# Taps and operand sums one product later, operand tiles at one offset from the weights, and an ordered end of the last stage

## The chip, the cores and the metric

The kernel runs on one core of a Trainium2 chip. The metric is the device time of one execution in microseconds (us). TensorE (PE) multiplies, VectorE (DVE) and ScalarE (ACT) do elementwise work, SyncE (SP) issues most transfers, and GpSimd (POOL) issues the transfers that add to what is already in the destination.

## The reference, cut to what matters

One layer of a hybrid encoder on 512 tokens of 2048 channels, float32:

```python
h = rms_norm(x, norm_mix_w); proj = h @ w_in            # attention and gated linear attention
x = x + concat([y_a, y_g]) @ w_out                      # stage "wo"
h = rms_norm(x, norm_ffn_w)
u = causal_depthwise_conv(h @ w_ffn_up, w_conv, b_conv) # stage "up": width 3, 2 * 5632 channels
u_gate, u_val = split(u, 2)
x = x + (gelu(u_gate) * u_val) @ w_ffn_down             # stages "dn0", "dn1", "dn2"
h = rms_norm(x, norm_ple_w)
x = x + sigmoid(h @ w_ple_gate) * (p @ w_ple_proj)      # stage "pg"
out = rms_norm(x, final_norm_w)
```

## The kernel before, in words

**Two parts.** Up to about 630 us the kernel does the input projection and both kinds of attention. Then `p @ w_ple_proj` is made ("pp"), and the six stages above follow as one list of steps. Only this list and its end are touched by the change, apart from where some tiles lie.

**Units and products.** A stage is a list of units: wo 8, up 44, dn0, dn1 and dn2 8 each, pg 8, 84 in all. A unit makes two blocks of 128 output channels for two halves of 256 tokens, a two-by-two block product with seven multiplications in place of eight. The seven products P1, P2, P6, P5, P7, P3, P4 (lines 29 to 31) each take a combination of weight blocks (L11, L12, S2, S1, S3, S4, L22) and one of seven operands (R11, R21, N2, N1, T3, R22, T4). The last unit of pg has the order P1, P2, P6, P7, P4, P5, P3 (`HALVES`), so that its first token half is finished two products early. `product` (line 736) does 3 matmuls of 128x256 for each block of 128 inputs, high by high, high by low, low by high: 24 matmuls, or 21 in dn1 and dn2. The sums lie in three PSUM banks A, B and C. `collect` (line 755) moves a product out of its bank: the first of a quarter by ACT (P1, P6, P5, P4), the others by DVE (P2, P7, P3). A product that goes into a bank again has to wait until the last `collect` of this bank is done.

**What is done around a product.** At step i the program first does `prep(i + 2)` (line 714): a sum of weight blocks by DVE where one is needed ("s"), the high part of the weights by ACT ("wh") and the low part by DVE ("wl"). Then come the 24 matmuls of step i, then what the `agenda` has for this step, then `collect`. "wh" and "wl" have three pages each, so "wh" of step i+2 can't start before product i-1 is done. In the six stages PE, ACT and DVE run in program order (`InOrder`, line 54); the issue of transfers by SP and POOL is put in order by the framework.

**After a unit of up** (`after_up`, line 833), in the steps of the next unit. In the first step (P1): `scale` by DVE (u <- u,rb) and the last tap of both halves by ACT (cv <- u,cw). In the second (P2): two taps of the gate half by DVE. In the third (P6): GELU by ACT and two taps of the other half by DVE. In the fourth (P5): the product of both halves by DVE, and for every second unit `store_pair` (line 536): four operand sums by DVE (tp) and seven stores to DRAM (g_R, g_N, g_T). The first unit of such a pair leaves its result in its page until then.

**After a unit of pg** the gate is applied (`gate_steps`), the squares go to `acc`, and the result is stored (x3d). In the last unit six of these blocks are read back and weighted by ACT (`weigh`, 12 instructions of 128x512). Its end (lines 983 to 1002) is not in program order: mean square, square root, reciprocal and spreading over the partitions for each token half, a multiplication by DVE for each of 8 blocks, and 16 stores of 256 KB.

**Where tiles lie.** Weight pages "wh" and "wl" are 4096 bytes of each partition, a block of 128 columns is 512 bytes. The operand tiles are 8192 bytes; R11, R21 and N2 lie in the pool `xa` (line 523), which is laid from the top of the memory down, below the pool `late` (line 522); N1, T3, R22 and T4 lie in the pool `xb` (line 574) behind the pages and a tile `pad` of 32 bytes. In the allocation of the kernel before, every weight page begins at byte 3136 of a 4096-byte block, every `xb` tile at 3168, every `xa` tile at 4064; `xb` ends 896 bytes below `xa`. The attention part has tiles of its own in the same space: h, 4096 bytes each, begins at byte 3136 like the pages.

Of the kernel before, what the change touches and what calls it, by code (L numbers as in the profile page):

```python
# [39 lines left out]
def encoder_block(ctx: ExitStack, tc: tile.TileContext, A, out):  # L40
# [115 lines left out]
    def rstd_tok(parts, n, dst):  # L156
        nt = parts[0].shape[1] // P
        ms = psum_aux("ms")
        for t in range(nt):
            for i, sumsq in enumerate(parts):  # L160
                nc.tensor.matmul(ms[:, t:t + 1], sumsq[:, t * P:(t + 1) * P], ones[:, 0:1],
                                 start=i == 0, stop=i == len(parts) - 1)
        w = tp.tile([P, 3 * TT], F32, tag="tok", name="tok")
        a, y, t = w[:, 0:nt], w[:, TT:TT + nt], w[:, 2 * TT:2 * TT + nt]
        nc.vector.tensor_scalar(a, ms[:, 0:nt], 1.0 / n, EPS, ALU.mult, ALU.add)
        nc.scalar.activation(y, a, AF.Sqrt)
        nc.vector.reciprocal(y, y)
        nc.vector.tensor_tensor(t, y, y, ALU.mult)
        nc.vector.scalar_tensor_tensor(t, t, -0.5, a, ALU.mult, ALU.mult)
        nc.vector.scalar_tensor_tensor(dst, t, 1.5, y, ALU.add, ALU.mult)  # L170

    def rstd_bc(rt):
        nt = rt.shape[1]
        dg = tp.tile([P, T], F32, tag="dg", name="dg", bufs=1)
        for t in range(nt):
            nc.vector.tensor_scalar(dg[:, t * P:(t + 1) * P], ident, rt[:, t:t + 1], None, ALU.mult)
        pb = psum_aux("pb")[:, :nt * P]
        nc.tensor.matmul(pb, ones, dg[:, :nt * P], start=True, stop=True)
# [343 lines left out]
    late.append(ctx.enter_context(tc.tile_pool(name="late", bufs=1, side="right", reuse_waits="tile")))  # L522
    xa = ctx.enter_context(tc.tile_pool(name="xa", bufs=1, side="right", reuse_waits="tile"))
# [212 lines left out]
    def product(unit, prod):  # L736
# [9 lines left out]
        for k in range(kb):  # L746
            x = st.x[op, k // 4]
# [85 lines left out]
    def after_up(unit):  # L833
# [41 lines left out]
    def after_gate(unit):  # L875
        return gate_steps(unit) + [(3, lambda: nc.sync.dma_start(x3d[unit.u], unit.xs))]
# [67 lines left out]
    for m in range(6):  # L944
        agenda[end + 4 + m // 3].append((2, lambda m=m: weigh(m)))
# [9 lines left out]
    for i, (unit, prod) in enumerate(steps):  # L955
# [8 lines left out]
        prep(i + 2)  # L964
        product(unit, prod)
        for k, f in todo:
            if k:
# [3 lines left out]
        if unit is units[-1] and j == 6:  # L971
            for e in (vec, act, ten):
# [92 lines left out]
```

## Time and profile before

| | |
|---|---|
| time before, median of 3 runs | 2454.15 us (2450.79 to 2454.41) |
| the profiled execution's own time | 2446.06 us |
| its span, first to last instruction | 2444.3 us |
| mean granted clock of TensorE | 0.986 |
| first product of wo, up, dn0, dn1, dn2, pg | 671.0, 832.8, 1762.8, 1937.8, 2083.3, 2231.1 us |

The profile shows one execution. A row of the timeline holds: start in us, length in us, engine, line, operation, out <- in, tile, count, and in brackets how long the engine sat idle before it and what ended this. The in-order engines are recorded under line 62, since a helper issues their instructions; rows are told apart by their tiles (up_T is T3 or T4, up_R is R11, R21 or R22, by bank A, B or C). Matmuls overlap and their ends are modelled, so their pace is read from their starts. PEclk is the granted clock as a share of full speed.

### The profile page before, as it was taken

The page shows a single profiled execution, that of the slowest core. Times are in us where ns is not written, and L with a number is a line of the kernel's source. Part 1 is how long each engine was busy: PE and PEld are TensorE (multiplying, and loading weights), DVE is VectorE, ACT ScalarE, POOL GpSimd, SP SyncE. Part 2 cuts the span into 40 slices and gives each one's busy share as a digit, 9 for nine tenths or more (in the row PEclk, how much of TensorE's full clock was granted, in tenths as well). Part 3 has the DMA queues.
Part 4 walks back from the last instruction along what each step waited for, and adds up shares of the span by engine and source line. Part 5 has one row for each costly group of instructions (what it writes and reads, how often), then busy time and mean ns, then how long its engine had stood idle before and what let it go on. Part 6 is the DMA issues. An engine that isn't in the chain of part 4 may idle for free.

```text
span 2444.3 us, 42306 instructions
## 1 busy us (share of the span) xinstructions
PE 2346.1 (96%) x16904; PEld 2182.8 (89%) x16904; DVE 1795.8 (73%) x2436; ACT 1231.2 (50%) x1770; POOL 103.4 (4%) x133
## 2 busy tenths in 40 slices
PE   9999999999999899999999999999989999898995
PEld 8878887777799899999999999999989999898895
DVE  5355336665588888878878787878887887999786
ACT  6344235554465654554554545544554544656554
POOL 0000000000000000000000000000000000000000
PEclk9999999999999999999999999999989999999997
DMA  5222222223987967777777777777854846769564
GB/s 198 85 78 74 99 95 95 91 91 123 305 278 231 324 172 199 206 200 195 201 195 201 197 206 195 203 195 208 269 192 156 286 155 212 276 213 328 166 215 163
DMA packets 171653, 462.72 MB, mean 189 GB/s; under 512 B 18720, under 2 KB 62496, under 8 KB 171456
## 3 DMA queue, kind: packets, MB, share of 16 engines
q1 hardware_dynamic: 152288, 396.58, 46.3%
q0 software_dynamic: 16992, 61.35, 13.9%
q8 instruction: 132, 2.16, 0.3%
q10 hardware_dynamic: 2176, 2.10, 0.3%
q14 instruction: 65, 0.53, 0.1%
HBM read 383.41 MB, written 69.21 MB: 185 GB/s over the span
## 4 chain that ended last, share of the span: by engine, by line
PE 60%; DVE 17%; ACT 8%; issue 8%; DMA 6%; SPq 0%; ACTq 0%; DVEq 0%
PE accA L62 21%; PE accC L62 10%; DVE wl L62 5%; ACT wh L62 4%; PE accB L62 4%; DVE u L62 3%; DMA g_N<-tp 3%; DVE cv L62 3%; PE v L241 2%; PE v L242 2%; PE v L243 2%; DVE s L62 2%; ACT cv L62 1%; PE pqa L124 1%; PE pqa L123 1%
## 5 line engine op out<-in xcount | busy, mean ns | idle before, releaser
L62 DVE TENSOR_TENSOR wl<-s,wh 128x1024 fp32r<-128x1024 f32 (+1 forms) x304 | 364.9, 1200 | 249.5 <-ACT wh L62 247.0
L62 ACT ACTIVATE wh<-l 128x1024 fp32r<-128x1024 f32 (+1 forms) x284 | 294.0, 1035 | 247.3 <-PE accC L62 130.4
L62 DVE TENSOR_TENSOR wl<-l,wh 128x1024 fp32r<-128x1024 f32 (+1 forms) x284 | 338.7, 1193 | 42.9 <-ACT wh L62 40.7
L62 ACT ACTIVATE wh<-s 128x1024 fp32r<-128x1024 f32 (+1 forms) x304 | 310.2, 1034 | 36.7 <-DVE s L62 32.8
L62 PE MATMUL accA<-up_T,wh 128*128 128x256 f32 x1408 | 255.8, 281 | 12.6 <-DVE u L62 12.4
L62 PEld LDWEIGHTS accA<-up_T,wh 128*128 128x128 f32 x1408 | 215.9, 189 | 16.6 <-issue 16.2
L62 ACT ACTIVATE u<-accA 128x256 f32<-128x256 f32 x253 | 95.2, 376 | 257.7 <-PE accA L62 256.2
L62 PE MATMUL accA<-up_T,wl 128*128 128x256 f32 x704 | 201.6, 286 | 5.3
L62 DVE TENSOR_TENSOR s<-s,l 128x1024 f32<-128x1024 f32 (+1 forms) x168 | 200.6, 1194 | 4.8 <-DMA l<-in_w_out 2.7
L62 PEld LDWEIGHTS accA<-up_T,wl 128*128 128x128 f32 x704 | 132.9, 189 | 13.7 <-DVE wl L62 13.7
L62 PE MATMUL accA<-up_N,wh 128*128 128x256 f32 x704 | 132.6, 289 | 3.8 <-ACT u L62 3.4
L62 DVE SCALAR_TENSOR_TENSOR cv<-u,cw,cv 128x511 f32<-128x511 f32 (+1 forms) x176 | 131.7, 748 | 3.1
L62 PE MATMUL accA<-up_R,wh 128*128 128x256 f32 x704 | 128.9, 283 | 4.6 <-DVE up_R L62 2.3
L62 PE MATMUL accA<-dn_T,wh 128*128 128x256 f32 x704 | 127.5, 281 | 1.8 <-DVE dn_T L62 1.8
L62 PE MATMUL accB<-up_R,wh 128*128 128x256 f32 x704 | 128.2, 282 | 0.2 <-DVE up_R L62 0.2
L62 PE MATMUL accC<-up_N,wh 128*128 128x256 f32 x704 | 125.6, 279 | 1.8 <-DVE up_N L62 1.8
L62 PE MATMUL accC<-up_R,wh 128*128 128x256 f32 x704 | 125.5, 279 | 0.1
L62 ACT ACTIVATE cv<-u,cw 128x512 f32<-128x512 f32 x88 | 67.0, 809 | 110.3 <-DVE u L62 110.3
L62 PEld LDWEIGHTS accA<-up_N,wh 128*128 128x128 f32 x704 | 108.7, 190 | 10.9 <-ACT u L62 6.0
L62 PEld LDWEIGHTS accA<-up_R,wh 128*128 128x128 f32 x704 | 108.9, 190 | 5.5 <-DVE up_R L62 2.5
L676 POOL DMA_DIRECT2D s<-in_w_up x88 | 75.0, 852 | 852.1 <-DMA s<-in_w_up 423.5
L62 PEld LDWEIGHTS accA<-dn_T,wh 128*128 128x128 f32 x704 | 108.3, 189 | 3.0 <-DVE dn_T L62 2.8
(369 smaller groups left out, 6486.9 us busy)
## 6 DMA issues: line engine op xcount, KB each, us to landing
l<-in_w_up SPq DMA_DIRECT2D x132, 512.0 KB, 6.5
s<-in_w_up SPq DMA_DIRECT2D x88, 512.0 KB, 4.2
s<-in_w_up POOLq DMA_DIRECT2D x88, 512.0 KB, 7.2
l<-in_w_dn SPq DMA_DIRECT2D x60, 448.0 KB, 5.0
l<-in_w_ple_gate SPq DMA_DIRECT2D x32, 512.0 KB, 5.8
l<-in_w_out SPq DMA_DIRECT2D x30, 512.0 KB, 5.5
l<-in_w_dn SPq DMA_DIRECT2D x30, 512.0 KB, 4.9
g_R<-cv SPq DMA_DIRECT2D x66, 128.0 KB, 6.6
```

Of the source, the lines that this page charges most:

```text
L62: ins = f(*args, **kw)
L123: nc.tensor.matmul(po, whi, act[:, 0, :], start=start, stop=False)
L124: nc.tensor.matmul(po, whi, act[:, 1, :], start=False, stop=False)
L241: nc.tensor.matmul(ps[t], h1[kt][:, 0, sl], wh, start=kt == 0, stop=False)
L242: nc.tensor.matmul(ps[t], h1[kt][:, 0, sl], wl, start=False, stop=False)
L243: nc.tensor.matmul(ps[t], h1[kt][:, 1, sl], wh, start=False, stop=kt == KD - 1)
L676: nc.gpsimd.dma_start(t, src("L22" if name == "S1" else "L11"), accum_op=ALU.add)
```

## The change

The two taps by ACT go from the first step to the second, and the operand sums with their stores (`join`) from the fourth to the fifth. A tile `shim` of 960 bytes is put into the pool `late`, ahead of `xa`. The tile "rt" with its two buffers of 32 bytes, which lay below the weight pages, is no longer there. At the end, all three engines stay in program order to the last instruction; the last product is cut after 5 of its 8 blocks for the mean square of the first token half; two of the eight blocks are weighted in the final multiplication and no longer by ACT; the other weightings are spread over more steps; the store of the last but one unit, which nothing read, is left out.

```diff
     late.append(ctx.enter_context(tc.tile_pool(name="late", bufs=1, side="right", reuse_waits="tile")))
+    shim = late[0].tile([P, 240], F32, tag="shim", name="shim")
+    nc.gpsimd.memset(shim, 0.0)
     xa = ctx.enter_context(tc.tile_pool(name="xa", bufs=1, side="right", reuse_waits="tile"))
...
-    def product(unit, prod):
+    def product(unit, prod, at=None, between=None):
...
         for k in range(kb):
+            if k == at:
+                between()
...
         def gate():
             g = unit.c[:, 1, :]
             vec.tensor_tensor(g, unit.c[:, 0, :], g, ALU.mult)
+
+        def join():
             ci, k, second = unit.slot
-            if not second:
-                held[0] = g
+            if second:
+                store_pair(gd[ci], k, held[0], unit.c[:, 1, :])
             else:
-                store_pair(gd[ci], k, held[0], g)
-
-        return [(0, scale), (0, lambda: tap(0, 2)), (0, lambda: tap(1, 2)), (1, lambda: [tap(0, 1), tap(0, 0)]),
+                held[0] = unit.c[:, 1, :]
+
+        return [(0, scale), (1, lambda: [tap(0, 2), tap(1, 2)]), (1, lambda: [tap(0, 1), tap(0, 0)]),
                 (2, lambda: act.activation(unit.c[:, 0, :], unit.c[:, 0, :], AF.Gelu_apprx_tanh)),
-                (2, lambda: [tap(1, 1), tap(1, 0)]), (3, gate)]
+                (2, lambda: [tap(1, 1), tap(1, 0)]), (3, gate), (4, join)]
...
     def after_gate(unit):
-        return gate_steps(unit) + [(3, lambda: nc.sync.dma_start(x3d[unit.u], unit.xs))]
+        keep = [] if unit is units[-2] else [(3, lambda: nc.sync.dma_start(x3d[unit.u], unit.xs))]
+        return gate_steps(unit) + keep
...
-    for m in range(6):
-        agenda[end + 4 + m // 3].append((2, lambda m=m: weigh(m)))
+    for m in range(4):
+        agenda[end + 3 + m // 2].append(((1, 3, 1, 1)[m], lambda m=m: weigh(m)))
...
+        if i == len(steps) - 1:
+            break
         product(unit, prod)
         for k, f in todo:
-            if k:
+            if 0 < k < 3:
                 f()
         if j == 6 and unit.first and st.chained:
             rstd_wide(acc, D, rb)
-        if unit is units[-1] and j == 6:
-            for e in (vec, act, ten):
-                e.on = False
         collect(unit, prod)
+        for k, f in todo:
+            if k == 3:
+                f()
         if unit is units[-1]:
             if prod == "P4":
-                for _, f in gate_steps(unit, lo_half):
+                for n, (_, f) in enumerate(gate_steps(unit, lo_half)):
                     f()
+                    if n == 1:
+                        weigh(4)
...
-    pb0 = rms_tokens([acc[:, lo_half]])
-    for _, f in gate_steps(unit, hi_half):
-        f()
-    pb1 = rms_tokens([acc[:, hi_half]])
-    for m in (6, 7):
-        x3[m] = units[m - 8].xs
-        weigh(m)
-    finish(lo_half, pb0)
-    finish(hi_half, pb1)
+    def finish(c, pb, ms):
+        for m in ms:
+            t = x3[m][:, :, c]
+            if m < 6:
+                vec.tensor_tensor(t, t, pb[:, None, :].broadcast_to([P, 2, 256]), ALU.mult)
+            else:
+                for s in range(2):
+                    vec.scalar_tensor_tensor(t[:, s, :], t[:, s, :], nfin[:, m + 8 * s:m + 8 * s + 1], pb,
+                                             ALU.mult, ALU.mult)
             (nc.sync if m % 2 else nc.scalar).dma_start(out2[m][:, :, c], t)
+    got = []
+    product(unit, prod, 5, lambda: got.append(mean_square(lo_half)))
+    w0 = rstd_begin(got[0])
+    collect(unit, prod)
+    x3[6], x3[7] = units[-2].xs, unit.xs
+    c = hi_half
+    o, xs = unit.o[:, :, c], unit.xs[:, :, c]
+    vec.tensor_tensor(o, o, rb[:, None, c].broadcast_to([P, 2, 256]), ALU.mult)
+    act.activation(o, o, AF.Sigmoid)
+    weigh(5)
+    r0 = rstd_end(w0)
+    pb0 = spread(r0, lo_half)
+    vec.tensor_tensor(o, o, unit.pp[:, :, c], ALU.mult)
+    vec.tensor_tensor(xs, xs, o, ALU.add)
+    sqs = []
+    for s in range(2):
+        q = tp.tile([P, T], F32, tag="sq", name="sq")[:, c]
+        act.activation(q, xs[:, s, :], AF.Square)
+        sqs.append(q)
+    finish(lo_half, pb0, range(1))
+    for q in sqs:
+        vec.tensor_tensor(acc[:, c], acc[:, c], q, ALU.add)
+    ms1 = mean_square(hi_half)
+    finish(lo_half, pb0, range(1, 2))
+    w1 = rstd_begin(ms1)
+    finish(lo_half, pb0, range(2, 3))
+    r1 = rstd_end(w1)
+    pb1 = spread(r1, hi_half)
+    finish(lo_half, pb0, range(3, 8))
+    finish(hi_half, pb1, range(8))
```

`mean_square` is two matmuls of `acc` with a column of ones, `rstd_begin` one DVE instruction and the square root by ACT, `rstd_end` four small DVE instructions, `spread` two DVE instructions and one matmul.

More of the change, by code (lines that the diff above doesn't have):

```diff
@@ L175, in rstd_bc @@
         for t in range(nt):
[L176 removed]
+            vec.tensor_scalar(dg[:, t * P:(t + 1) * P], ident, rt[:, t:t + 1], None, ALU.mult)
         pb = psum_aux("pb")[:, :nt * P]
[L178 removed]
+        ten.matmul(pb, ones, dg[:, :nt * P], start=True, stop=True)
         return pb
@@ new lines, in rstd_end, with spread @@
+    def rstd_end(w):
+        a, y, t, r = (w[:, 2 * q:2 * q + 2] for q in range(4))
+        vec.reciprocal(y, y)
+        vec.tensor_tensor(t, y, y, ALU.mult)
+        vec.scalar_tensor_tensor(t, t, -0.5, a, ALU.mult, ALU.mult)
+        vec.scalar_tensor_tensor(r, t, 1.5, y, ALU.add, ALU.mult)
+        return r
+    def spread(r, c):
+        dg = tp.tile([P, T], F32, tag="dg", name="dg", bufs=1)[:, c]
+        for t in range(2):
+            vec.tensor_scalar(dg[:, t * P:(t + 1) * P], ident, r[:, t:t + 1], None, ALU.mult)
+        tag = 3 * ((unit.index + 1) % 2) + c.start // 256
+        pb = pp_.tile([P, T], F32, tag=f"b{tag}", name="pb")[:, :256]
+        ten.matmul(pb, ones, dg, start=True, stop=True)
+        return pb
```

31 lines of the change are left out of this document (17 added, 14 removed).

## The prediction

> **What bounds the kernel now.** I read the page first, then the timeline of PE alone, then those of DVE and ACT in the same stretches. The page says 96% for PE, but a matmul's length is modelled, so I go by starts. Four steps of a unit of wo (the fourth row is the start of P5), then the start of the next unit:
>
> ```profile
> 753.48 0.40 PE L62 MATMUL accA<-wo_R,wh 128*128 128x256 f32 x2
> 756.36 0.40 PE L62 MATMUL accB<-wo_R,wh 128*128 128x256 f32 x2
> 759.24 0.40 PE L62 MATMUL accA<-wo_N,wh 128*128 128x256 f32 x2
> 762.12 0.40 PE L62 MATMUL accC<-wo_N,wh 128*128 128x256 f32 x2
> 773.32 0.40 PE L62 MATMUL accA<-wo_R,wh 128*128 128x256 f32 x2
> ```
>
> Nothing waits here. P1, P2 and P6 take 2.88 us each, the other four (773.32 - 762.12) / 4 = 2.80. That is 120.0 against 116.7 ns for a matmul of one form, and the slow three read the tiles of `xa`. A unit takes 19.84 us; with seven fast products it would take 19.60.
>
> Now up: the starts of its third unit and of dn0, and between them one pair of units (P1, P7, P3, P4, then the next two P1).
>
> ```profile
> 890.95 0.40 PE L62 MATMUL accA<-up_R,wh 128*128 128x256 f32 x2
> ...
> 1015.43 0.40 PE L62 MATMUL accA<-up_R,wh 128*128 128x256 f32 x2
> ...
> 1026.96 0.39 PE L62 MATMUL accA<-up_T,wh 128*128 128x256 f32 x2
> ...
> 1030.16 0.39 PE L62 MATMUL accC<-up_R,wh 128*128 128x256 f32 x2
> ...
> 1033.70 0.47 PE L62 MATMUL accA<-up_T,wh 128*128 128x256 f32 x2 [0.57 <-DVE u L62]
> ...
> 1036.57 0.40 PE L62 MATMUL accA<-up_R,wh 128*128 128x256 f32 x2
> ...
> 1056.91 0.40 PE L62 MATMUL accA<-up_R,wh 128*128 128x256 f32 x2
> ...
> 1762.83 0.39 PE L62 MATMUL accA<-dn_R,wh 128*128 128x256 f32 x2
> ```
>
> The pair takes 41.48 us (21.14 + 20.34) against 39.20 at full pace. P7 takes 1030.16 - 1026.96 = 3.20, so it waits 0.40 inside; P4 starts 3.54 after P3, so it waits 0.74 for DVE's `collect`. All 42 units from the third on take 871.88 us, 20.76 each. PE is the bound in wo and dn; in up the order of DVE and ACT costs it over 1 us a unit. The rows of the second unit (ACT, then DVE, then three DVE rows of the pair's first):
>
> ```profile
> 1040.54 1.52 ACT L62 ACTIVATE cv<-u,cw 128x512 f32<-128x512 f32 x2 [2.43 <-DVE u L62]
> 1041.96 0.36 ACT L62 ACTIVATE u<-accA 128x256 f32<-128x256 f32 x1
> 1042.23 2.00 ACT L62 ACTIVATE wh<-s 128x1024 fp32r<-128x1024 f32 x2
> ```
>
> ```profile
> 1039.28 1.22 DVE L62 TENSOR_TENSOR u<-u,rb 128x1024 f32<-128x1024 f32 x1
> 1043.31 1.23 DVE L62 TENSOR_TENSOR wl<-s,wh 128x1024 fp32r<-128x1024 f32 x1 [2.80 <-ACT wh L62]
> ...
> 1047.36 1.22 DVE L62 TENSOR_TENSOR wl<-s,wh 128x1024 fp32r<-128x1024 f32 x1
> ```
>
> ```profile
> 1030.53 0.76 DVE L62 TENSOR_TENSOR tp<-cv 128x256 f32<-128x256 f32 x2
> ...
> 1033.14 0.41 DVE L62 TENSOR_TENSOR u<-u,accA 128x256 f32<-128x256 f32 x1
> ```
>
> ACT waits 2.43 us for `scale`, does both taps, only then collects P1 and makes wh of P5; DVE, done with `scale` at 1040.5, sits idle 2.80 us for that wh. The lost time comes back as P7's wait: its wl starts at 1047.36, and P7 is due 11.3 us after 1036.57, at 1047.9. In the pair's other unit the four operand sums and one wl hold DVE from 1030.53 to 1033.14, so `collect` of P7 comes late for P4.
>
> **The taps and the sums.** Nothing is added: two taps (0.76 us each) move from step P1 to step P2 on ACT, four sums from P5 to P7 on DVE. I write out a unit from its start 0, with products 2.80 long, DVE at 1.15 between starts of 128x1024 instructions, 0.76 a tap and 1.00 for a wh. P2 starts at 2.80, P6 5.60, P5 8.40, P7 11.20, P3 14.00, P4 16.80. ACT: `collect` P1 at 3.0, wh of P5 3.3 to 4.3, taps 4.3 to 5.8, wh of P7 to 6.8, GELU when its taps are there, 7.0 to 7.8. DVE: `scale` 2.7 to 3.9, wl of P5 4.3 to 5.5, two taps to 7.0, `collect` P2 7.4, s to 8.5, wl of P7 8.5 to 9.7 (due 11.4), two taps to 11.2, wl of P3 12.4 (due 14.2), gate 13.0, wl of P4 14.2. Then in every second unit the sums, 1.46, to 15.7, and `collect` P7 to 16.0, due 16.8. The next wl are done at 17.2 and 19.7, due 19.8 and 22.6. Nothing is late; the smallest slack is the 0.8 us at P4. The total doesn't bind either:
>
> ```profile
> 990.28:1745.02 754.74, 739.17 (x6110) 722.92 (x6109) 607.85 (x729) 374.29 (x507) 61.33 (x72) 1.00 0.72 202
> ```
>
> Over these 36 units of up (columns PE, weight loads, DVE, ACT, POOL, clock, DMA share, GB/s) DVE works 607.85 / 754.74 = 0.81 of the time, 33.4 us of a pair, and 39.2 are there.
>
> So each of the 42 units comes to 19.60 us if the operands are all fast: 871.88 - 823.2 = **48.7**. If the `xa` operands stay slow, up to 0.24 a unit is left as in wo, 10 us in all; in the unit of 20.34 only 0.34 is over when 19.60 and P7's 0.40 are taken off, with other small waits in it, so I take half, 5 us less.
>
> Two stretches of another kind gain by the same edit:
>
> ```profile
> 875.51 0.80 PE L62 MATMUL accA<-up_N,wh 128*128 128x256 f32 x2 [3.36 <-ACT u L62]
> ```
>
> ```profile
> 1771.53 1.52 ACT L62 ACTIVATE cv<-u,cw 128x512 f32<-128x512 f32 x2 [4.93 <-DVE u L62]
> ```
>
> ```profile
> 1774.29 1.23 DVE L62 TENSOR_TENSOR wl<-s,wh 128x1024 fp32r<-128x1024 f32 x1 [2.80 <-ACT wh L62]
> ```
>
> In up's second unit `collect` of P1 stands behind the taps, which wait for the first norm, and P6 waits 3.36 us and more for it. Out of that order, P6 waits for its own wl, and P7 for the GELU's table and its wl: I take 3.9 us, between 3 and 4.9. In dn0's first unit DVE is the bound, splitting operands, and loses 2.80 us behind the taps of up's last unit. That goes, and the sums fall behind one split: **3** us, between 1.5 and 4.
>
> **The offset.** What is in question is whether the place of a tile can cost PE 2.8%. Rows of before show it. First vproj (h and weights 0 bytes apart, modulo 512), then the small gate product, whose weights step 32 columns, 128 bytes, for every second matmul (line 293), with h as before:
>
> ```profile
> 88.06 0.39 PE L241 MATMUL v<-wv_h,h 128*128 128x512 f32 x1
> ...
> 94.86 0.39 PE L294 MATMUL plr<-h,glh 128*128 128x512 f32 x1
> 95.08 0.40 PE L295 MATMUL plr<-h,glh 128*128 128x512 f32 x1
> 95.32 0.40 PE L294 MATMUL plr<-h,glh 128*128 128x512 f32 x1
> 95.56 0.40 PE L295 MATMUL plr<-h,glh 128*128 128x512 f32 x1
> 95.80 0.40 PE L294 MATMUL plr<-h,glh 128*128 128x512 f32 x1
> ...
> 96.72 0.39 PE L294 MATMUL plr<-h,glh 128*128 128x512 f32 x1
> ```
>
> 30 matmuls of vproj take 6.80 us, 227 ns each; the gate product goes 0.22, then 0.24 three times, then 0.92 for the next four. Same engine, same h, only the weights' address modulo 512 differs, and a matmul costs up to 0.24. So the distance counts, not the tile's place in the memory. Weights less operand is 3136 - 4064, or 96 modulo 512, for `xa`, and 3136 - 3168, or 480, for `xb`. After the change, without rt's 64 bytes, pages stand at 3072 and `xb` at 3104; `xa` goes down by 960 to 3104, and the gap of 896 + 64 is just the shim. All tiles then have the distance of `xb`, which the trace shows at 116.7 ns. Outside up that is 0.24 us for each unit that doesn't wait: 7 in wo (1.7) and 7 in dn0 (1.7), 21/24 of it for 14 in dn1 and dn2 (2.5 by wo's size; I take 2.4), 0.1 for 6 in pg, which wait a little for ACT (0.6, between 0 and 0.24 each), and as an estimate 0.9 for pp, whose 95 wide matmuls read a tile of `xa` (line 560), and for first units: **7.3** us. At the other bound it is nothing.
>
> [...]
>
> **The end.**
>
> ```profile
> 2414.99 1.01 PE L161 MATMUL ms<-ones,acc 128*128 128x1 f32 x4 [4.31 <-DVE acc L62]
> ```
>
> ```profile
> 2416.01 5.34 PE accC L62 x24
> ```
>
> ```profile
> 2416.00:2421.00 5.00, 5.00 (x25) 5.00 (x24) 0.33 (x2) 4.70 (x7) 0.00 (x0) 0.50 0.00 0
> 2440.00:2442.00 2.00, 0.00 (x0) 0.00 (x0) 0.00 (x0) 0.00 (x0) 0.00 (x0) 0.50 1.03 343
> ```
>
> ```profile
> 2424.09 1.29 DVE L991 TENSOR_TENSOR x<-x,pb 128x512 f32<-128x512 f32 x2 [0.79 <-PE pb L178]
> ```
>
> ```profile
> 2435.58 2.77 ACTq L992 DMA_DIRECT2D out<-x  x3
> ```
>
> PE idles 4.31 us for the first half's sum of squares ahead of the last product, which then runs at clock 0.50 (5.34 us in place of 2.80) to 2421.35. After the change 15 of its matmuls (1.75 us) run first, from 2410.7 to 2412.4. The sum is ready as before: as many weightings stand ahead of it on ACT, save one that fills idle time. So PE idles 2.6 us, does the mean square (0.5) and the last 9 (1.05) at full clock, and ends at 2416.5. From there to the second spread DVE has, one after the other, `collect` 0.4, gate 0.6, root 0.8, spread 0.5, gate 1.2, a square 0.7 (ACT), the sums 0.75, three blocks of the first half at 0.60, root 0.9, spread 0.5, and PE 1.2: 9.3 us, 2425.8. Then 13 blocks are left, 5 of the first half from 2425.1 on. The rows give 343 GB/s, 0.76 us for 256 KB; the last 8 stores now take 2444.3 - 2435.58 = 8.72, which is 8 x 0.76 and 2.6 of start and close. With 13 it is 2425.1 + 9.9 + 2.6 = 2437.6. That is 6.7 us less than 2444.3; if the clock still drops, 1.05 for the 9 matmuls and some for the small ones go. I take **6**, between 4.5 and 7. The store that goes was beside all this and counts nothing, and so does the memset on POOL, once and long before its space is used.
>
> [...]
>
> **The sum**: 48.7 + 3.9 + 3 + 7.3 + 6 = 68.9 us of the profiled execution's 2446.06, so 2377.2. The measured median stands 8.09 above that execution; I carry this over: **2385**.
>
> **The rivals.**
>
> *The offset counts for nothing* (the change then doesn't do what it says in this part, or the tiles come to lie elsewhere). Against it stand the rows of the gate product; for it, that I infer from 512-wide matmuls. It gives back 7.3 and about 5 of up: 2397. [...]
>
> *One wait stays in up*, the one with the least slack, P4 behind the sums, now at step P7. For it: 0.8 us is little over some 30 instructions, and faster products leave DVE less time. Against it: the same durations put the waits of before in the right places. If it stays whole, 21 times 0.74 to 0.8: 2402. If it shrinks by half, 2394.
>
> *Slower: the weights come late.* The seven stores of a pair are issued by SP 2.9 us later, and SP's loads for the coming units queue behind them. The tightest is S3, an SP load with a POOL transfer that adds to it:
>
> ```profile
> 1048.29 0.86 POOL L676 DMA_DIRECT2D s<-in_w_up  x1 [6.02 <-DMA s<-in_w_up]
> ```
>
> ```profile
> s<-in_w_up POOLq DMA_DIRECT2D x88, 512.0 KB, 7.2
> ```
>
> It lands at 1055.5; its wh is the second of the two from 1042.23, at 1043.2, in the next unit 20.3 later, so 1063.5. Slack 8 us. Only a delay of over 8 us in every pair makes PE wait, and 69 / 21 = 3.3 us more bring the kernel to where it was; at 12.5 us of delay it is some 25 us slower, 2480. The stores move by 2.9, and wl of P5, whose end frees the page for S3, comes 2.5 earlier. Hence unlikely.
>
> **How the numbers follow.** The forecast, all parts as worked out: 0.65. Offset nothing: 0.12. A wait that stays: 0.15. More than forecast, by over 10 us (other waits in first units go as well): 0.04. Slower: 0.04. The range has to hold the forecast with its bounds (3.9, 3 and 6 at their low ends lose 3.9, at their high ends gain 3; the runs of before spread by 3.6, and the 8.09 may not carry over), and the next two rivals: 2374 to 2404. About 0.2% is what a measurement of this kernel can tell from no change. Of the third case 0.02 falls within it; so faster 0.94, same 0.02, slower 0.04.
>
> **What would show it.** In the timeline of PE every product of up starts 2.80 after the last, P1, P2 and P6 among them, in wo and dn too; no P7 or P4 of up waits. DVE's idle 2.80 before wl is 0.4. P6 of up's second unit comes some 3 us earlier. The last product runs at clock 1.00, and the last 13 stores follow each other at 0.76. If P1, P2 and P6 stay at 2.85 to 2.88, the offset was wrong; if P4 still has "DVE u" before it, the slack was; if ACT's wh waits for "DMA s", the stores were in the way.

## The result, and the profile after

The changed kernel takes **2392.51 us** by the median of four runs (2386.41 to 2403.76), the kernel before 2453.9 (2450.79 to 2454.41, four runs): a ratio of 0.9758, with a 95% interval of 0.9717 to 0.9798. Forecast were 2385 and a range of 2374 to 2404. The time lies inside the range, and 61.4 us were gained of the 68.9 forecast. Two things were not foreseen: the runs spread over 17 us, where the four of before spread over 4 (and the 15 of before that ran beside e10_sums over 10), and the end of the kernel gained less than half of what I gave it.

The profiled execution is the longest of the four (2403.76, span 2402.1), so its trace shows losses that other runs don't have. First the busy time by stretches (from:to, length; PE, weight loads, DVE, ACT, POOL; clock, DMA share, GB/s): wo from its third unit, up from its third unit, dn0 from its second.

```profile
720.67:841.63 120.96, 120.96 (x1010) 120.96 (x1009) 96.59 (x119) 65.36 (x93) 6.82 (x8) 1.00 0.81 244
897.38:1728.42 831.04, 831.04 (x7059) 831.04 (x7058) 713.00 (x843) 446.46 (x592) 71.73 (x84) 1.00 0.78 213
1760.51:1897.71 137.20, 137.20 (x1179) 137.20 (x1177) 104.94 (x106) 62.94 (x81) 3.41 (x4) 1.00 0.58 193
```

In all three PE is busy for the whole length; no product of up waits. The 42 units of up take 831.04 us, against 871.88 before. But they are not alike: a unit is 168 matmuls, so one takes 120.96 / (6 x 168) = 120.0 ns in wo, 831.04 / (42 x 168) = 117.78 in up, 137.20 / (7 x 168) = 116.67 in dn0. Within a stretch all seven products go at one pace, P1, P2 and P6 like the others (2.88 us each in wo, 2.80 in dn0). The forecast had 116.67 in all.

The order of up is as worked out. ACT in one unit (`collect` of P1, wh of P5, the taps), then DVE (wl of P5):

```profile
1038.91 0.39 ACT L62 ACTIVATE u<-accA 128x256 f32<-128x256 f32 x1 [1.49 <-PE accA L62]
1039.19 1.06 ACT L62 ACTIVATE wh<-s 128x1024 fp32r<-128x1024 f32 x1
1040.14 1.51 ACT L62 ACTIVATE cv<-u,cw 128x512 f32<-128x512 f32 x2
```

```profile
1040.28 1.23 DVE L62 TENSOR_TENSOR wl<-s,wh 128x1024 fp32r<-128x1024 f32 x1 [0.47 <-ACT wh L62]
```

The taps wait for nothing (before 2.43 us), and DVE's 2.80 us ahead of this wl are 0.47.

The last unit starts at 2352.54. Its end, on PE and on DVE, and three stretches:

```profile
2375.76 0.72 PE L62 MATMUL accC<-pg_R,wh 128*128 128x256 f32 x2 [4.58 <-DVE u L62]
...
2379.05 0.59 PE L62 MATMUL ms<-ones,acc 128*128 128x1 f32 x4
```

```profile
2374.32 0.96 DVE L62 TENSOR_TENSOR acc<-acc,sq 128x256 f32<-128x256 f32 x2 [0.48 <-ACT sq L62]
2375.20 0.41 DVE L62 TENSOR_TENSOR u<-u,accC 128x256 f32<-128x256 f32 x1
```

```profile
2371.00:2375.70 4.70, 0.18 (x2) 0.00 (x0) 3.30 (x7) 3.66 (x6) 0.00 (x0) 1.00 0.00 0
2376.00:2378.90 2.90, 2.90 (x15) 2.90 (x15) 0.00 (x0) 0.00 (x0) 0.00 (x0) 0.50 0.00 0
...
2392.00:2400.00 8.00, 0.00 (x0) 0.00 (x0) 5.58 (x12) 0.00 (x0) 0.00 (x0) 0.50 1.04 350
```

PE still idles for 4.58 us, now ahead of the last product (P3) instead of ahead of the mean square, and runs P3's first part at clock 0.50. From the last unit's start to the end of the span it takes 49.5 us; before it was 52.3.

The terms of the sum, each as the difference of the stretch's length, in the first profile and in the second one of the same kernel (e1_again, below):

| stretch | forecast | first profile | e1_again |
|---|---|---|---|
| up to wo's first product, and up's first unit | -0.9 | +6.3 | +2.7 |
| wo | -1.7 | +3.8 | -1.5 |
| up's second unit | -3.9 | -3.7 | -3.8 |
| up's other 42 units | -48.7 | -40.8 | -48.7 |
| dn0's first unit | -3 | -4.1 | -3.8 |
| dn0's other units | -1.7 | -1.6 | -1.6 |
| dn1 and dn2 | -2.4 | 0.0 | -1.5 |
| pg but its last unit | -0.6 | +0.6 | -0.5 |
| from the last unit's start on | -6 | -2.7 | -1.6 |
| sum | -68.9 | -42.2 | -60.4 |

### The profile page after: what moved, and what is told of

It reads as the page before. It is cut to its first block, busy times and chain, and to the rows that moved or that the text cites. A ratio compares the mean times of both kernels' runs of the same rounds, so it can differ in the third digit from the quotient of the medians.

```text
span 2402.1 us, 42280 instructions
## 1 busy us (share of the span) xinstructions
PE 2324.5 (97%) x16904; PEld 2178.9 (91%) x16904; DVE 1807.5 (75%) x2440; ACT 1236.5 (51%) x1766; POOL 104.0 (4%) x134
## 4 chain that ended last, share of the span: by engine, by line
PE 85%; DVE 5%; DMA 5%; ACT 2%; issue 2%; SPq 0%; DVEq 0%; POOL 0%; ACTq 0%; POOLq 0%
PE accA L62 35%; PE accC L62 17%; PE accB L62 8%; PE v L241 2%; PE v L242 2%; PE v L243 2%; PE pqa L124 1%; PE pqa L123 1%; PE pka L125 1%; DMA dn_N<-g_N 1%; PE pqa L125 1%; PE pka L123 1%; PE pka L124 1%; DVE wl L62 1%; PE py L497 1%
## 5 line engine op out<-in xcount | busy, mean ns | idle before, releaser
L62 ACT ACTIVATE wh<-s 128x1024 fp32r<-128x1024 f32 (+1 forms) x304 | 315.6, 1038 | 15.9 <-DVE s L62 12.1
L62 PE MATMUL accA<-up_N,wh 128*128 128x256 f32 x704 | 126.6, 280 | 0.4 <-DVE up_N L62 0.4
L62 PEld LDWEIGHTS accC<-up_N,wh 128*128 128x128 f32 x704 | 108.7, 189 | 2.1 <-DVE up_N L62 2.1
L62 PEld LDWEIGHTS accB<-up_R,wh 128*128 128x128 f32 x704 | 108.7, 189 | 0.8 <-DVE up_R L62 0.8
```

The lines of the kernel that those rows point to most:

```text
L62: ins = f(*args, **kw)
```

## The experiments

Each kernel ran beside the kernel before on the same chip (medians of before: 2452.3 to 2452.7). From here on a distance in bytes is operand less weights, modulo 512: `xb` and, after the change, `xa` stand at 32, and `xa` of before at 416. (The prediction took weights less operand, which gave 480 and 96; that is the other way round.) The table has them all; "42 units" is up from its third unit in the profiled run.

| kernel | median us (lowest to highest) | 42 units | last unit's start to the end |
|---|---|---|---|
| e1_again: the changed kernel again | 2391.4 (2385.59 to 2396.3) | 823.20 | 50.7 |
| e2_noshim: without the offset | 2403.95 (2398.37 to 2405.84) | 833.19 | 50.9 |
| e3_offset: before, with the offset alone | 2449.62 (2444.99 to 2457.46) | 872.35 | 52.2 |
| e4_zero: all tiles at 0 bytes | 2425.28 (2424.13 to 2426.25) | 846.72 | 49.3 |
| e5_collect: `collect` of P5 earlier | 2385.56 (2384.77 to 2387.6) | 823.20 | 45.8 |
| e6_whole: and the mean square after P3 | 2387.38 (2384.94 to 2391.16) | 823.20 | 44.7 |
| e7_d64: all tiles at 64 bytes | 2401.96 (2400.28 to 2404.34) | 831.04 | 50.6 |
| e8_d480: all tiles at 480 bytes | 2407.89 (2406.34 to 2410.27) | 834.96 | 50.5 |
| e9_taps: sums back, taps late | 2391.12 (2390.78 to 2399.69) | 823.19 | 50.3 |
| e10_sums: taps back, sums late | 2446.33 (2444.33 to 2450.52) | 872.95 | 49.4 |
| e11_d96: e6_whole at 96 bytes | 2420.63 (2417.76 to 2424.96) | 846.72 | 44.9 |
| e12_mixed: e6_whole, one tile at 416 | 2386.56 (2384.86 to 2387.75) | 824.88 | 44.7 |

**Which of the two moves freed up?** One of them undone at a time, in the changed kernel. e9_taps puts the sums back:

```diff
-                (2, lambda: [tap(1, 1), tap(1, 0)]), (3, gate), (4, join)]
+                (2, lambda: [tap(1, 1), tap(1, 0)]), (3, gate), (3, join)]
```

> The changed kernel with the four operand sums (and their stores) back in the step of the gate product; the taps stay one product later. My theory: the waits of up (P7 for its wl, P4 for DVE) are both worked up from the taps, since ACT collects P1 and makes the wh of P5 behind them and DVE loses 2.80 us for it; with the taps later, DVE has the time for the sums in either step. By the schedule that I wrote out by hand a pair takes 39.2 to 39.7 us at 116.67 ns a matmul, so the 42 units from the third on take 823 to 834 us, and no more than 0.5 us a pair is waited for; by the median 2386 to 2404, as the changed kernel. Rival: the sums are what delays P4, and their step matters by itself; then P4 waits 0.74 in every pair and up takes 15 us more, 838 to 850.

e10_sums puts the taps back:

```diff
-        return [(0, scale), (1, lambda: [tap(0, 2), tap(1, 2)]), (1, lambda: [tap(0, 1), tap(0, 0)]),
+        return [(0, scale), (0, lambda: tap(0, 2)), (0, lambda: tap(1, 2)), (1, lambda: [tap(0, 1), tap(0, 0)]),
```

> The changed kernel with the taps back in the step of P1 and ahead of P1's collect on ACT; the operand sums stay one product later. My theory: nearly all of up's gain is the taps' and is lost here: DVE waits 2.80 us for the wh of P5 again and P7 comes 0.4 us late for its wl; the sums, one step later, then keep DVE from a collect one step later. By the hand schedule a pair takes 41.5 us, as in before (41.48), and the 42 units some 872 us: 2433 to 2445 by the median. Up's second unit takes 25 us again (before 24.99, changed 21.2) and dn0's first 35 to 36 (before 36.18, changed 32). Rival: taps and sums each remove one of the two waits; then P7's 0.4 in each unit stays and P4's 0.74 goes: 40.0 to 40.4 a pair, 840 to 850 in all, 2405 to 2420.

The 42 units of e9_taps, then those of e10_sums, then ACT's taps and DVE's wl of P5 in a unit of e10_sums:

```profile
889.79:1712.98 823.19, 823.19 (x7058) 823.19 (x7057) 709.56 (x843) 444.39 (x592) 71.72 (x84) 1.00 0.77 214
```

```profile
891.61:1764.56 872.95, 854.60 (x7058) 833.93 (x7057) 701.98 (x842) 437.80 (x592) 71.72 (x84) 1.00 0.74 203
```

```profile
1041.40 1.52 ACT L62 ACTIVATE cv<-u,cw 128x512 f32<-128x512 f32 x2 [2.43 <-DVE u L62]
```

```profile
1044.17 1.23 DVE L62 TENSOR_TENSOR wl<-s,wh 128x1024 fp32r<-128x1024 f32 x1 [2.81 <-ACT wh L62]
```

It is the taps alone. With the sums in their old step nothing waits: 823.19 us, 39.2 a pair. With the taps in their old step the 2.43 and the 2.81 us are back and a pair takes 872.95 / 21 = 41.57 (41.48 before); the hand schedule had said 41.5. P4 of every second unit waits as it did before, 3.53 us behind the start of P3 (1072.59 to 1076.12; DVE's `collect` of P7 ends at 1075.97), though the sums stand one step later. Up's second unit is back at 25.2 us and dn0's first at 35.7; the median, 2446.33, lies just above the range that I had written down. So the rival, by which each move takes one wait away, falls, and the sums' move is worth nothing that shows: the changed kernel has 2391.4 (e1_again) and 2392.5 with it, e9_taps 2391.12 without. The stores that follow the sums matter as little.

**What is the offset worth?** e2_noshim takes the offset alone out of the changed kernel; e3_offset puts it alone into the kernel before.

```diff
-    shim = late[0].tile([P, 240], F32, tag="shim", name="shim")
-    nc.gpsimd.memset(shim, 0.0)
...
+    rt = tp.tile([P, TT], F32, tag="rt", name="rt")
+    nc.gpsimd.memset(rt, 0.0)
```

> The changed kernel with the offset alone undone: the shim is gone and the 64 bytes that the change freed are taken again, so that every tile stands where it stood before; the order of up and the end are those of the changed kernel. My prediction's theory (the distance of 416 makes the three products on xa slow): wo 19.84 a unit, up 19.84 (3 products of 2.88, four of 2.80), dn0 19.84: outside up some 7 us and in up 10 us more than at 116.67 throughout. Against the first profile of the changed kernel, whose up took 19.79 and whose wo took 20.16, that is about +2 in up, -2 in wo, +2 in dn0, +2 in dn1 and dn2: 2392 to 2400 by the median. If the distance counts for nothing, xa and xb take the same pace here too, and the time is that of the changed kernel within its spread. Either way no product of up waits for DVE or ACT; if P7 or P4 wait again, the order was not what removed the wait.

```diff
+    shim = late[0].tile([P, 224], F32, tag="shim", name="shim")
+    nc.gpsimd.memset(shim, 0.0)
     xa = ctx.enter_context(tc.tile_pool(name="xa", bufs=1, side="right", reuse_waits="tile"))
```

> The kernel before with the offset alone: a shim of 896 bytes puts xa at 3168 modulo 4096, where xb is, 32 bytes behind the pages; the order of up and the end are unchanged. My prediction gave the offset 7.3 us outside up and nothing in up as long as products wait there: 2446.6 by the median, with all seven products of wo and dn0 at 2.80. By what the first profile of the changed kernel shows, the seven get one pace, but not always the quick one: with 120.0 in wo it is 2.2 us slower there than before, with 116.67 it is 1.7 quicker, and so for each stage: between 2444 and 2462. In up the waits of P7 and P4 stay, 20.7 to 20.8 a unit. If a wait sets the pace anew each time, up's units differ among themselves.

Up in e2_noshim, then in e3_offset:

```profile
893.17:1726.36 833.19, 833.19 (x7058) 833.19 (x7057) 712.91 (x843) 447.11 (x592) 71.54 (x84) 1.00 0.77 212
```

```profile
893.91:1766.26 872.35, 852.83 (x7059) 832.12 (x7058) 701.73 (x842) 437.57 (x592) 71.55 (x84) 1.00 0.74 203
```

Without the offset up goes without a wait too, at 833.19 / 42 = 19.84 a unit: that is three products at 120.0 ns and four at 116.67, as in wo of before (119.04 us for 6 units, 19.84 each). So the taps alone are worth 871.88 - 833.19 = 38.7 us here. The median is 12.5 us above e1_again, and above the 2392 to 2400 that I had expected; the prediction had 7.3 outside up and about 5 in up. In the kernel before, the offset alone gives 2.8 us (ratio 0.9987, interval 0.9978 to 0.9997): up still waits, and outside it this run drew 116.67 in wo and 117.8 in dn0, dn1 and dn2. I had written down 7.3.

**Is the pace fixed by the distance?** e1_again is the changed kernel as it stands; the others change the pad and the shim together, so that all tiles keep one distance (e4_zero has no pad and a shim of 248; e8_d480 a pad of 120 and a shim of 128):

```diff
-    shim = late[0].tile([P, 240], F32, tag="shim", name="shim")
+    shim = late[0].tile([P, 232], F32, tag="shim", name="shim")
...
-    pad = xb[0].tile([P, 8], F32, tag="pad", name="pad")
+    pad = xb[0].tile([P, 16], F32, tag="pad", name="pad")
```

> The changed kernel once more, not a letter different. In its first profile all seven products of a unit run at one pace, but the pace is 120.0 ns a matmul in wo, 117.78 in up and dn1, 116.67 in dn0 and dn2, though the distance between weights and operand is 32 bytes throughout. Theory 'layout': addresses and the stage's form fix the pace; then this profile shows 120.0, 117.78, 116.67, 117.78, 116.67 again, up's third to last unit take 19.79 us each, and the runs lie within some 4 us as those of before did. Theory 'mode': PE settles into one of several steady paces when a stretch begins and keeps it until something makes it wait; then other stages have other paces this time. Up's 42 units are 7056 matmuls, so 116.67 there is 7.8 us less than in the first profile, 120.0 is 15.7 us more, and the runs spread over more than 10 us, as the first four did (2386 to 2404). The 5 us that the stretch before wo was longer: under both theories they are chance, and are not there in every run.

> The changed kernel with all operand tiles 0 bytes from the weights modulo 4096 instead of 32: the 32-byte pad is gone and the shim is 32 bytes longer. In before, vproj with distance 0 and a gate product at distance 0 were the quickest rows (227 ns). Theory 'distance': 0 is as good as or better than 32, and each stage goes at 116.67: up 19.60, wo 19.60, 2384 by the median with a spread of a few us. Theory 'mode': the same set of paces as with 32 (116.67, 117.78, 120.0), drawn again by stage: 2386 to 2404, with a spread over 10 us. If 32 bytes are what lets PE read both at once, 0 is slower in every stage: 120 or more, 2412 and up.

> The changed kernel with all operand tiles 64 bytes behind the weights modulo 4096 (pad 64, shim 928), in place of 32. So far: 0 bytes gave 120.0 ns a matmul in every stage of e4_zero and four runs within 2.2 us; 32 bytes gave 116.67, 117.78 or 120.0, another in each stage and run, and spreads of 10 to 17 us; 416 bytes (xa of before) 118 to 120, and xb at 32 behind it always 116.67. Theory 'distance picks a set of paces': 64 has a set of its own, and if it holds one pace only the runs lie within 4 us: near 2385 if that is 116.67, near 2425 if it is 120. Theory '0 is special, all else alike': the same draws as at 32, 2385 to 2404 with a spread of 10 us.

> The changed kernel with all operand tiles 480 bytes behind the weights modulo 4096, that is 32 ahead of the next step of 512. If the absolute value of the distance counts, it is as 32: 116.67, 117.78 or 120.0 by stage, 2385 to 2404 with a spread over 10 us. If the sign counts (PE reads a weight column of 512 bytes and an operand row of 1024 bytes in step, and one has to be ahead of the other), it is a set of its own: 120 throughout gives 2425, 116.67 throughout 2385, each with a spread below 4 us.

e1_again in the three stretches of the first table, then the 42 units of e4_zero, e7_d64 and e8_d480:

```profile
716.41:834.01 117.60, 117.60 (x1011) 117.60 (x1010) 96.88 (x120) 66.20 (x93) 6.81 (x8) 1.00 0.83 253
888.31:1711.51 823.20, 823.20 (x7058) 823.20 (x7057) 710.44 (x843) 444.73 (x592) 71.54 (x84) 1.00 0.78 215
1743.87:1881.07 137.20, 137.20 (x1178) 137.20 (x1177) 105.12 (x106) 62.98 (x81) 3.40 (x4) 1.00 0.58 193
```

```profile
894.64:1741.36 846.72, 846.72 (x7059) 846.72 (x7057) 713.23 (x843) 446.55 (x592) 71.56 (x84) 1.00 0.76 209
```

```profile
893.38:1724.42 831.04, 831.04 (x7059) 831.04 (x7058) 712.76 (x843) 445.65 (x592) 71.55 (x84) 1.00 0.77 213
```

```profile
892.20:1727.16 834.96, 834.96 (x7059) 834.96 (x7058) 712.82 (x843) 446.36 (x592) 71.55 (x84) 1.00 0.77 212
```

e1_again, the same kernel with the same addresses, runs wo and up at 116.67 ns (117.60 and 823.20 us), where the first profile had 120.0 and 117.78. Theory "layout" falls. At 0 bytes it is 120.0 in wo, up and all of dn (dn0 takes 141.12 us behind its first unit, dn1 and dn2 123.48 each), at 64 bytes 117.8 in wo, up, dn0 and dn1, at 480 bytes 118.3 in wo, up, dn0 and dn2 (in dn1 PE waits 1.9 us), and the runs of each lie within some 4 us; only at 32 bytes are there several paces, and the quickest is among them. So the distance decides which paces there are. 32 bytes are the only distance of those tried at which PE kept 116.67 through whole stages, and it does so by chance: of the five kernels with all tiles at 32 in which nothing waits in up, four ran up at 116.67 in their profile and one at 117.78. My guess that 0 is as good or better, drawn from wider matmuls, was wrong: 2425 in place of 2384.

**Why did the end give so little?** P3 adds into the bank that `collect` of P5 reads, and that `collect` stood on DVE behind the first half's gate product and sums. e5_collect moves it into the gap (0.69 us in the changed kernel) in which DVE waits for the sigmoid; e6_whole also puts the mean square behind the whole of P3.

```diff
             if prod == "P4":
-                for n, (_, f) in enumerate(gate_steps(unit, lo_half)):
-                    f()
-                    if n == 1:
-                        weigh(4)
+                half = [f for _, f in gate_steps(unit, lo_half)]
+                half[0]()
+                half[1]()
+                weigh(4)
+            elif prod == "P5":
+                for f in half[2:]:
+                    f()
```

> The changed kernel with one thing moved on DVE: the collect of P5 in the last unit stands ahead of the first half's gate product and sums, in a gap of 0.69 us in which DVE waits for the sigmoid. Theory 'bank' (what failed in my step on the end): P3 adds into the bank that P5's collect reads, and DVE came to that collect only at 2375.6, so PE idled 4.58 us and ran the last product at clock 0.50. Then here PE idles some 1.2 us before P3, the first 15 matmuls run at clock 1.00 and are over before the sum of squares is ready, the mean square follows it at once, and P3 ends some 3.5 us earlier against the unit's start: 24.5 to 25 us in place of 28.2. The end of the span follows by 3.5 us, 46 us after the unit's start in place of 49.56. Rival: the first half's sums set the end, and P3 goes at the old time; then nothing changes by over 0.5 us. By the median 2388 (the changed kernel has 2391 to 2393), with the spread of 10 us that it has itself; the stretch of the last unit tells more than the median.

```diff
-    got = []
-    product(unit, prod, 5, lambda: got.append(mean_square(lo_half)))
-    w0 = rstd_begin(got[0])
+    product(unit, prod)
     collect(unit, prod)
+    w0 = rstd_begin(mean_square(lo_half))
```

> As e5_collect, and the mean square of the first half stands behind the whole last product instead of inside it. P3 then runs through without a gap, ends about when the sum of squares is ready, and DVE collects P3 1 to 2 us earlier than in e5_collect; the first half's root is no later. If the 13 blocks that are stored after the second root set the end, it comes 1 to 1.5 us earlier than in e5_collect; if the 16 stores from the first one on set it (0.76 us each, 12.2 us and 2.6 of start and close behind the first block), it ends with e5_collect, since the first block is no earlier.

e5_collect: P3 and the mean square on PE, `collect` of P5 on DVE, and the stretch of P3's first part. Then PE in e6_whole.

```profile
2359.73 0.47 PE L62 MATMUL accC<-pg_R,wh 128*128 128x256 f32 x2 [1.03 <-DVE u L62]
...
2362.86 0.61 PE L62 MATMUL ms<-ones,acc 128*128 128x1 f32 x4 [1.14 <-DVE acc L62]
```

```profile
2359.17 0.41 DVE L62 TENSOR_TENSOR u<-u,accC 128x256 f32<-128x256 f32 x1
```

```profile
2359.70:2362.00 2.30, 1.99 (x15) 1.81 (x15) 1.53 (x3) 2.05 (x5) 0.00 (x0) 1.00 0.00 0
```

```profile
2358.43 0.48 PE L62 MATMUL accC<-pg_R,wh 128*128 128x256 f32 x2 [1.02 <-DVE u L62]
...
2361.56 0.60 PE L62 MATMUL ms<-ones,acc 128*128 128x1 f32 x4
```

PE's 4.58 us are 1.03, P3 runs at clock 1.00 and ends 24.5 us after the unit's start (28.3 in the changed kernel), and the span ends 45.8 us after it: as theory "bank" had said (24.5 to 25, and 46). With the mean square after P3 it is 44.7, another 1.1. This doesn't tell the 13 late blocks from the 16 stores, as I had meant it to: `collect` of P3, which stands on DVE ahead of most of the first half's root, no longer waits there for the end of P3, so the first block is multiplied 27.1 us after the unit's start in place of 28.2, earlier by the same 1.1. By the medians e5_collect is 2385.56, all five runs below 2387.7, and ahead of the changed kernel (2391.4 and 2392.5) as well as of the kernel before (ratio 0.9727, interval 0.9714 to 0.9741). e6_whole, whose end is quicker, has a higher median, 2387.38, with runs 6 us apart: with such a spread a median of four runs can't show 1.1 us.

**Another distance, or another way to the quick pace?** Both of these stand on e6_whole. e11_d96 has a pad of 24 and a shim of 248 - 24 = 224. e12_mixed leaves thirteen tiles at 32 bytes and puts the first half of P6's at 416:

```diff
-    shim = late[0].tile([P, 240], F32, tag="shim", name="shim")
+    shim = late[0].tile([P, 144], F32, tag="shim", name="shim")
...
+            if op == "N2" and g == 0:
+                gap = xa.tile([P, 96], F32, tag="gap", name="gap")
+                nc.gpsimd.memset(gap, 0.0)
             stages[0].load(op, g)
```

> The kernel of e6_whole with all operand tiles 96 bytes behind the weights modulo 4096 in place of 32 (pad 96, shim 896). Paces by distance so far: 0 gives 120.0 ns everywhere, 64 gives 117.8 everywhere, 480 gives 118.2 to 118.4, 416 117 to 120, and 32 mostly 116.67 with draws of 117.75 and 120. If 96 behaves as 32 does, since it differs from it by 64, the stages draw from 116.67, 117.75 and 120: 2382 to 2398. If every multiple of 32 has a pace of its own, it is one pace throughout and runs within 4 us: 2383 at 116.67, 2395 at 117.8, 2400 at 118.3, 2417 at 120. The stretch behind the last unit's start stays at 44.7 us, save 0.15 for the pace.

> The kernel of e6_whole with one of the fourteen operand tiles, the first half of P6's, at 416 bytes from the weights (where all of xa stood in before) and the thirteen others at 32. What is open is which pace PE keeps at distance 32. With all tiles at 32 a stage goes at 116.67, 117.75 or 120.0 throughout; with xa at 416 (before, and e2_noshim) the tiles at 32 went at 116.65 in nearly all units, whatever the stage. Theory 'the tile ahead sets it': coming from a tile at 416 PE falls into the quick pace and keeps it until the next unit's P6. Then 12 of a unit's 168 matmuls take 119 to 120 and 156 take 116.65: 19.64 us a unit of 8 blocks in wo, up and dn0 and none at 19.79 or 20.16; with 0.04 a unit 3 us more than an all-quick run, some 2387 by the median, and the runs lie within 4 us where e6_whole had 6 and the changed kernel 10 to 17. Theory 'drawn at a stretch's start': some stage goes at 117.75 or 120 again outside P6, and the spread stays. Rival: 12 slow matmuls are not enough, or throw PE into the slow pace for all the rest, 2400 and more.

Wo in e3_offset, and wo and up in e11_d96; then up and dn0 in e12_mixed, and the starts of P1, P6 and P5 of its second unit of wo and of the next P1:

```profile
717.40:835.00 117.60, 117.60 (x1010) 117.60 (x1009) 96.58 (x119) 66.17 (x93) 6.81 (x8) 1.00 0.84 251
```

```profile
716.98:837.93 120.95, 120.95 (x1010) 120.95 (x1009) 96.56 (x119) 66.02 (x93) 6.82 (x8) 1.00 0.81 244
893.20:1739.92 846.72, 846.72 (x7059) 846.72 (x7058) 712.81 (x843) 446.92 (x592) 71.72 (x84) 1.00 0.76 209
```

```profile
890.61:1715.49 824.88, 824.88 (x7059) 824.88 (x7058) 712.10 (x843) 444.05 (x591) 71.56 (x84) 1.00 0.77 214
1748.79:1886.27 137.48, 137.48 (x1179) 137.48 (x1178) 105.10 (x105) 63.01 (x81) 3.40 (x4) 1.00 0.58 192
```

```profile
698.56 0.41 PE L62 MATMUL accA<-wo_R,wh 128*128 128x256 f32 x2
...
704.33 0.40 PE L62 MATMUL accA<-wo_N,wh 128*128 128x256 f32 x2
...
707.17 0.40 PE L62 MATMUL accC<-wo_N,wh 128*128 128x256 f32 x2
...
718.47 0.40 PE L62 MATMUL accA<-wo_R,wh 128*128 128x256 f32 x2
```

96 bytes are as bad as 0: 846.72 is 120.0. The median, 2420.63, lies 3.6 us above what I had written down for that pace, and the four runs spread over 7.2 us although wo, up and dn all go at 120.0 in the profile; so a spread alone is no sign of several paces. e11_d96 and e3_offset also settle whether the distance counts or the operand's own place: in both the operand tiles begin at byte 3168 of a 4096-byte block, the weights at 3072 in the one and at 3136 in the other, and wo takes 120.95 us at 96 and 117.60 at 32. e12_mixed goes as the first of its theories said: 824.88 / 42 = 19.64 a unit. The unit of wo shows it at work: P1 and P2 go at (704.33 - 698.56) / 48 = 120.2 ns, the pace drawn at the start of the stretch; from P5 on it is (718.47 - 707.17) / 96 = 117.7, and the six units behind average 19.64 us. The tile at 416 costs 0.04 us a unit and brings PE out of a slow pace, in one or two units. Dn0, dn1 and dn2 fit this: behind their first units they take 137.48, 120.21 and 120.46 us, 116.9, 116.8 and 117.1 ns a matmul with P6 among them, where the changed kernel kept 117.8 through all of dn1 (121.19 us). The runs lie within 2.9 us, but so do those of e5_collect (2.8), which has no such tile, so their spread proves nothing. The median, 2386.56, is that of e5_collect and e6_whole within their spread; what it has over the changed kernel is mostly the end (44.7 us against 49.5 and 50.7).

## Why the prediction held, and where it didn't

**The taps and the sums** held as a size: 48.7 us where up drew the quick pace, 40.8 in the first profile, in which it drew 117.78 (7056 matmuls at 1.11 ns more are 7.8). The taps held as a mechanism too: they alone give 38.7, and the other 10.0 (833.19 - 823.20) come from the offset in up, twice the 5 us that I gave it there. The hand schedule got the state with the taps back within 0.1 us a pair. What didn't hold is the sums' part: the prediction priced both moves together and put P4's wait down to the sums, but with the taps late P4 waits in neither step of the sums (823.20 and 823.19 us, PE busy throughout), and with the taps early in both (it starts 3.54 and 3.53 us after P3). Up's second unit (3.8 for 3.9) is right, and dn0's first (3.8 to 4.1 for 3) lies at the upper bound of 4.

**The offset** came out right in size, 12.5 us by the medians for 7.3 and about 5, but that is partly luck: where up drew the quick pace the offset gave 10.0 there and not 5, where it drew 117.78 only 2.2 (833.19 - 831.04). As a rule it was wrong. The step that failed: "All tiles then have the distance of `xb`, which the trace shows at 116.7 ns." In before the `xb` products came behind products at 416 bytes, and from these PE went into the quick pace in the units that don't wait (2.80 us for a product on `xb` in wo, 2.45 for its 21 matmuls in dn1), as e12_mixed shows for a single such tile (120.2 ns ahead of it, 117.7 behind it); with all tiles alike nothing did that, and up kept its 117.78 over 7056 matmuls. Hence wo at 120.0 and up at 117.78 in the first profile, and at least part of the spread. The rival "the offset counts for nothing" is refuted by e2_noshim, and by e4_zero in the other direction: a distance can also cost 34 us (2425.28 against 2391.4), 23.5 of them in up's 42 units (846.72 us at 0 bytes, 823.20 at 32).

**The end** was mis-sized: 6 forecast, 2.7 and 1.6 measured. The step that failed: "After the change 15 of its matmuls (1.75 us) run first, from 2410.7 to 2412.4." I had followed P3's operands but not its bank: P3 waits for `collect` of P5 (the 4.58 us), and the change had put the first half's sums ahead of that on DVE. The stall didn't go; it went over to P3. The sum also had the last 9 matmuls at full clock behind 2.6 us of idling, which no run shows: P3's first part went at clock 0.50 behind 4.58 us in the changed kernel and at 1.00 behind 1.03 us in e5_collect. With `collect` moved, the end gains 6.5 us against before (52.3 to 45.8): the forecast's 6 is what the order gives once that wait is gone.

**One wait stays in up** and **the weights come late**: neither. In up's 42 units P4 has no wait in e1_again, nor in e9_taps with the sums in their old step, and no wh of the changed kernel waits for a transfer (in up they wait 129.8 us in all, for PE and DVE alone).

**The 8.09 us** between profile and median were carried over as if they were a constant. They are not: after the change the first profile lies 11 us above its median and the second 6 below. To add them is the same as to take the 68.9 off the median of before. The 7.5 us between 2385 and 2392.5 are then the end (some 4) and, by the two profiles, the stages that went slower than the quick pace; which paces the other runs drew, no trace shows.

The stretch ahead of wo is longer in all profiles behind the first (673.0 to 676.0, before 671.0), also in e3_offset, which has the order of before, and in e2_noshim, which has its addresses. So neither the order nor the offset of the change accounts for it; with a single profile of before, more can't be said.

## What to carry over

When a wait is taken away by reordering, write down for the instruction that comes to stand first all that it waits for: operands, and the buffer that it writes to, with its reader's place in that reader's program order. When a layout gives one tile a better pace, repeat the run of the kernel as it is before the gain is put down to the layout, since a pace can depend on what ran ahead of the tile, as it did here (120.2 ns ahead of the tile at 416 bytes, 117.7 behind it). And undo each half of a double move by itself: here one half was worth all of it.

## What the runs showed of the hardware

The pace of 128x256 matmuls, each with weights of its own, in units that wait for nothing, by the distance (operand less weights) in bytes modulo 512. That 512 is the right step to count by was not tested.

| 0 | 32 | 64 | 96 | 416 (some tiles, others at 32) | 480 |
|---|---|---|---|---|---|
| 120.0 ns | 116.67, 117.78 or 120.0 | 117.8 | 120.0 | 117 to 120 | 118.3 |

At 32 a pace was held over 42 units, 7056 matmuls; it changed from stage to stage (120.0 in wo, 117.78 in up, 116.67 in dn0 of the changed kernel) and behind a tile at another distance (120.2 to 117.7 in e12_mixed). What draws it at a stretch's start, and why these distances have these paces, stays open; how PE reads weights and operand, of which the expectations of e4_zero and e8_d480 suppose something, no run shows. Other multiples of 32 weren't tried.

The granted clock changed three times at the changed kernel's end, 3.41 us apart. Three short stretches of it, and one of e6_whole's:

```profile
2375.50:2376.00 0.50, 0.24 (x1) 0.27 (x2) 0.11 (x1) 0.40 (x1) 0.00 (x0) 0.81 0.00 0
...
2379.00:2379.40 0.40, 0.40 (x6) 0.40 (x4) 0.00 (x0) 0.00 (x0) 0.00 (x0) 0.72 0.00 0
...
2382.40:2382.80 0.40, 0.00 (x0) 0.00 (x0) 0.33 (x3) 0.40 (x2) 0.00 (x0) 0.79 0.00 0
```

```profile
2364.60:2365.00 0.40, 0.29 (x2) 0.00 (x0) 0.40 (x1) 0.40 (x1) 0.00 (x0) 0.80 0.00 0
```

The clock (the third number from the end of a row) is a mean over the stretch. A mean of 0.81 over 0.5 us, if it goes from 1.00 to 0.50 in one step, puts the fall at 2375.81; the rise lies at 2379.22 and the next fall at 2382.63, 3.41 us apart each time. Ahead of the second fall PE had been idle for only 1.8 us (since 2380.80) and busy for the rest of the 3.41, as far as the modelled ends of matmuls tell; in e6_whole the clock falls at 2364.84, while a matmul is running, with some 1.3 us of work in the 3.41 before it. So a fall came behind 1.8 us of idling, less than the 2.6 behind which the sum had PE at full clock. What sets a fall off, these rows don't tell.
